# A two-layer hybrid trunk with experts: weights laid out row by row for their transfers, and the split of the experts' weights left to VectorE

## The chip, the cores and the metric

The kernel runs on one core of one Trainium2 chip. The core has a matrix engine (TensorE, PE in the rows; its weight loads are PEld), three engines for elementwise work (VectorE = DVE, ScalarE = ACT, GpSimd = POOL), a queue engine (SyncE = SP) that issues most transfers, and 16 DMA engines that move data between device memory (DRAM) and the core's memory (SBUF). The metric is device microseconds of one execution. Before the change the median of 3 runs is 2021.1 us (2020.6 to 2021.52).

## The reference

Two layers work on 256 tokens of 1024 channels. Each layer has a mixing part (dilated attention and a gated delta rule, both fed by one input projection, merged by gates, then an output projection and a layer norm) and a channel part. The channel part of layer 0 is a dense SwiGLU. That of layer 1 sends each token to 2 of 8 experts:

```python
def swiglu(x, w_gate, w_up, w_down):
    return (jax.nn.silu(x @ w_gate) * (x @ w_up)) @ w_down
...
    for e in range(N_EXPERTS):
        y = y + gates[..., e:e + 1] * swiglu(x, w_gate[e], w_up[e], w_down[e])
```

An expert has three matrices of 1024 x 3584 (the last one transposed), in float32. All 8 experts are computed, so 352 MB of their weights pass through the core once, beside some 144 MB of weights of the two mixing parts and of the dense channel part.

## The kernel before, in words

**Weights.** All weights go through one object, `Stream` (`W`). They are cut into pieces of two blocks of 128 rows and 512 columns: 128 partitions x 2 x 512 float32, 512 KB. `plan` lists the pieces in the order of their use. For each piece:

- `dma_to` issues the transfer on SP, into a 4 KB-per-partition slot named `raw` (L82). In DRAM the weights lie as the reference has them, so a partition of a piece is two runs of 2 KB. In the experts' part every third piece (`n_dma % HALVES == 0`) goes instead into two 2 KB slots named `rawh`, by two transfers of 256 KB (L79).
- `advance` splits the float32 values exactly into a high part `whi` (a float32r copy by ScalarE, L102 for a whole piece, L100 twice for a `rawh` piece) and a low part `wlo` (raw minus high, L105). For a whole piece VectorE does L105 once over 128x1024. For a `rawh` piece VectorE does the first half and GpSimd the second, 128x512 each. The same sharing, on whole slots, is used for every piece while `share` is set, which is the case from the output projection of layer 1 to the end of the first gate product of the experts' part.
- `gemm` (L414 to L416) makes three products for each block of 128 rows: high x by high w, high x by low w, low x by high w. So one piece is 2 x 3 products of 512 columns for each tile of tokens. In the experts' part an expert has one tile of at most 128 tokens; the mixing parts have two tiles.

`caps(raw, spl)` bounds how many pieces are loaded ahead (raw) and how many are split ahead (spl). In the experts' part they are (18, 5), then (21, 5). The slots come from two pools: `k4` with 36 slots of 4 KB (raw, whi, wlo, the gathered tokens `xe`, the hidden values `hte`, the split copies of x) and `k2` with 16 slots of 2 KB (rawh, `mgs`, the one-hot rows `Pt`, and others).

**The experts' part.** An expert's 3584 hidden columns are taken in 7 chunks of 512. A chunk is 12 pieces: 4 of gate (result `mg`), 4 of up (`mu`), and 4 of down (`oe`) for the chunk before. When `mu` is complete, VectorE multiplies it into `mgs` (L1322), TensorE turns `mgs` in four transposes (`ht`, L1335), and ScalarE and VectorE split that into `hte` (L1338, L1339), which the down products of the chunk read. At an expert's end `scatter` scales its two result halves (L1348 on ScalarE, L1349 on VectorE, `oh` and `ol`), two products per tile spread them over the tokens (`sc`, L1353 and L1354), and VectorE adds them to x (L1356). For every second expert the tokens of the next pair are gathered (`xe`, L1286).

**Order.** The program is written as one main line of products and a set of generators that are stepped between them; a scheduler then fixes each engine's order when the kernel is built. Every engine works through its own list in order and waits on semaphores. A change of what one engine does can therefore move instructions on the others.

The functions that the change touches, with what calls them:

Of the kernel before, what the change touches and what calls it, by code (L numbers as in the profile page):

```python
# [18 lines left out]
P = 128  # L19
# [24 lines left out]

class Stream:
    """Weights in the order of their use, in pieces of two row blocks: DRAM to SBUF, then their float32 values
    split exactly into two float32r parts. caps() bounds the pieces loaded ahead and those split ahead."""

    def __init__(self, k, raw, spl):
        self.k, self.raw_cap, self.spl_cap = k, raw, spl  # L50
        self.subs = []
        self.key = {}
        self.raw = {}
        self.split = {}
        self.n_dma = 0
        self.n_split = 0
        self.retired = 0
        self.done_subs = set()
        self.share = False
        self.moe = 0  # L60
        self.SHARE, self.HALVES = 3, 3

    def caps(self, raw, spl):
        self.raw_cap, self.spl_cap = raw, spl

    def add(self, key, src, kb, n):
        first = len(self.subs)
        for h in range(0, kb, 2):
            self.subs.append((src[:, h:h + 2], n))
        self.key[key] = list(range(first, len(self.subs)))  # L70

    def dma_to(self, i):
        while self.n_dma <= min(i, len(self.subs) - 1):
            src, n = self.subs[self.n_dma]
            q = self.k.nc.sync
            if self.n_dma >= self.moe and self.n_dma % self.HALVES == 0:
                t = [self.k.k2([P, 512], name="rawh") for _ in range(2)]
                for k in range(2):
                    q.dma_start(t[k][:, :n], src[:, k])  # L79
            else:  # L80
                t = self.k.k4([P, 2, 512], name="raw")
                q.dma_start(t[:, :, :n], src)  # L82
# [43 lines left out]
class Kern:  # L126
# [7 lines left out]
    # ---------------------------------------------------------------- interleaving  # L134
# [46 lines left out]
    # ---------------------------------------------------------------- small helpers  # L181
# [36 lines left out]
    # ---------------------------------------------------------------- constants  # L218
# [47 lines left out]
        # rows of an odd block of 16 and columns of the block before it  # L266
# [18 lines left out]
    def rope_tables(self):  # L285
        """cos and sin of position * frequency, with the angle reduced exactly by multiples of 2 pi."""
# [25 lines left out]
        # [c | c] and [-s | s]  # L312
# [33 lines left out]
    # ---------------------------------------------------------------- weight plan  # L346
    def plan(self):
        W, A = self.W, self.A

        def sq(w, r0, kb, c0, n):  # L350
            return w[r0 * P:(r0 + kb) * P, c0:c0 + n].rearrange("(k p) n -> p k n", p=P)

        for l in range(DEPTH):
            wi = A["w_in"][l]
            for kg in range(2):
                W.add(("at", l, 0, 0, kg), sq(wi, 4 * kg, 4, 0, 512), 4, 512)
            for half in range(2):
                for part in range(3):
                    for kg in range(2):
                        W.add(("qb", l, half, part, kg), sq(wi, 4 * kg, 4, C_QB + part * 1024 + half * 512, 512), 4, 512)  # L360
            for g in range(3):
                for part in range(1 if g == 0 else 0, 3):
                    for kg in range(2):
                        W.add(("at", l, g, part, kg), sq(wi, 4 * kg, 4, part * 1536 + g * 512, 512), 4, 512)
                for nm, c0 in ((("z", C_Z),), (), (("ga", C_GA), ("gb", C_GB)))[g]:
                    for f in range(2):
                        for kg in range(2):
                            W.add((nm, l, f, kg), sq(wi, 4 * kg, 4, c0 + f * 512, 512), 4, 512)
            for f in range(2):
                W.add(("ba", l, f, 0), sq(A["w_branch_a"][l], 0, 4, f * 512, 512), 4, 512)  # L370
                for kg in range(2):
                    W.add(("bb", l, f, kg), sq(A["w_branch_b"][l], 4 * kg, 4, f * 512, 512), 4, 512)
            for kg in range(2):
                for f in range(2):
# [1213 lines left out]
```

## Time and profile before

| | |
|---|---|
| median of 3 runs | 2021.1 us |
| profiled execution, first to last instruction | 2023.3 us |
| PE busy | 1960.1 us (97%) |
| PEld busy | 1640.3 us (81%) |
| DVE busy | 1644.2 us (81%) |
| ACT busy | 1270.8 us (63%) |
| POOL busy | 613.9 us (30%) |
| HBM read | 506.09 MB, 253 GB/s over the span |

The profile page is of one execution, whose span of 2023.3 us stands beside the 2021.1 us of the runs. The experts' part is the second half of the span: the rows of 40 slices show that DMA goes from about half busy to 9 tenths near slice 20, and that DVE goes up with it. A product's busy time in these rows (0.39 us) is longer than the distance from its start to the next one's start (0.23 us), because products are pipelined; distances between starts are read from the timeline.

### The profile page before, as it was taken

The page shows a single profiled execution, that of the slowest core. Times are in us where ns is not written, and L with a number is a line of the kernel's source. Part 1 is how long each engine was busy: PE and PEld are TensorE (multiplying, and loading weights), DVE is VectorE, ACT ScalarE, POOL GpSimd, SP SyncE. Part 2 cuts the span into 40 slices and gives each one's busy share as a digit, 9 for nine tenths or more (in the row PEclk, how much of TensorE's full clock was granted, in tenths as well). Part 3 has the DMA queues.
Part 4 walks back from the last instruction along what each step waited for, and adds up shares of the span by engine and source line. Part 5 has one row for each costly group of instructions (what it writes and reads, how often), then busy time and mean ns, then how long its engine had stood idle before and what let it go on. Part 6 is the DMA issues. An engine that isn't in the chain of part 4 may idle for free. (4 is left out here: it accounts for less than half of the span.)

```text
span 2023.3 us, 30086 instructions
## 1 busy us (share of the span) xinstructions
PE 1960.1 (97%) x10143; PEld 1640.3 (81%) x10143; DVE 1644.2 (81%) x2208; ACT 1270.8 (63%) x1958; POOL 613.9 (30%) x484
## 2 busy tenths in 40 slices
PE   8889999999999999999999999999999999999995
PEld 7878888888888878888788788887888878888784
DVE  7886757665566976666789989999899998999997
ACT  5554546444444555554388778777787777877784
POOL 4341211000003422210334334343343433434342
PEclk9899999999999999999999999999999999999998
DMA  8344344664664353537589999999999999999991
GB/s 297 105 157 150 132 132 154 197 222 131 236 215 127 118 177 95 181 127 239 205 292 373 354 350 347 363 366 350 350 357 359 366 355 334 371 358 370 351 351 42
DMA packets 278544, 513.65 MB, mean 254 GB/s; under 512 B 29904, under 2 KB 32176, under 8 KB 278384
## 3 DMA queue, kind: packets, MB, share of 16 engines
q1 hardware_dynamic: 276144, 504.11, 70.6%
q0 software_dynamic: 2240, 7.56, 1.1%
q8 instruction: 81, 1.33, 0.3%
q14 instruction: 79, 0.65, 0.1%
HBM read 506.09 MB, written 5.51 MB: 253 GB/s over the span
## 5 line engine op out<-in xcount | busy, mean ns | idle before, releaser
L105 DVE TENSOR_TENSOR wlo<-raw,whi 128x1024 fp32r<-128x1024 f32 (+1 forms) x726 | 921.7, 1291 | 121.4 <-ACT whi L102 118.5
L102 ACT CAST whi<-raw 128x1024 fp32r<-128x1024 f32 (+1 forms) x726 | 744.8, 1046 | 78.0 <-DVE wlo L105 18.9
L105 POOL TENSOR_TENSOR wlo<-rawh,whi 128x512 fp32r<-128x512 f32 x224 | 390.7, 1744 | 593.4 <-ACT whi L100 415.3
L105 DVE TENSOR_TENSOR wlo<-rawh,whi 128x512 fp32r<-128x512 f32 x224 | 269.1, 1201 | 6.3 <-ACT whi L100 6.3
L100 ACT CAST whi<-rawh 128x512 fp32r<-128x512 f32 x448 | 256.1, 622 | 18.8 <-PE mg L415 9.8
L415 PE MATMUL oe<-wlo,hte 128*128 128x512 f32 x448 | 180.7, 403 | 0.4
L415 PE MATMUL mu<-wlo,xe 128*128 128x512 f32 x440 | 172.6, 392 | 6.6 <-DVE wlo L105 6.3
L414 PE MATMUL oe<-whi,hte 128*128 128x512 f32 x448 | 175.7, 392 | 0.0
L416 PE MATMUL oe<-whi,hte 128*128 128x512 f32 x448 | 175.2, 391 | 0.0
L414 PE MATMUL mu<-whi,xe 128*128 128x512 f32 x440 | 171.6, 390 | 0.0
L416 PE MATMUL mu<-whi,xe 128*128 128x512 f32 x440 | 171.5, 390 | 0.0
L414 PE MATMUL mg<-whi,xe 128*128 128x512 f32 x440 | 171.4, 390 | 0.0
L416 PE MATMUL mg<-whi,xe 128*128 128x512 f32 x440 | 171.4, 390 | 0.0
L415 PE MATMUL mg<-wlo,xe 128*128 128x512 f32 x440 | 171.3, 389 | 0.0
L105 POOL TENSOR_TENSOR wlo<-raw,whi 128x512 fp32r<-128x512 f32 x53 | 84.3, 1603 | 102.5 <-ACT whi L102 84.0
L566 PE MATMUL qb<-xhl,whi 128*128 128x256 f32 x384 | 113.4, 296 | 0.0
L569 PE MATMUL qb<-xhl,whi 128*128 128x256 f32 x384 | 110.9, 289 | 0.0
L571 PE MATMUL qb<-xhl,wlo 128*128 128x256 f32 x384 | 110.8, 289 | 0.0
L414 PE MATMUL at<-whi,xhl 128*128 128x512 f32 x256 | 108.1, 422 | 0.0
L415 PE MATMUL at<-wlo,xhl 128*128 128x512 f32 x256 | 102.6, 401 | 3.3 <-DVE wlo L105 3.3
L415 PEld LDWEIGHTS mu<-wlo,xe 128*128 128x128 f32 x440 | 82.6, 188 | 28.4 <-DVE wlo L105 10.9
L416 PE MATMUL at<-whi,xhl 128*128 128x512 f32 x256 | 101.9, 398 | 0.0
(421 smaller groups left out, 3875.7 us busy)
## 6 DMA issues: line engine op xcount, KB each, us to landing
raw<-in_w_in SPq DMA_DIRECT2D x168, 512.0 KB
raw<-in_moe_w_gate SPq DMA_DIRECT2D x168, 512.0 KB
raw<-in_moe_w_up SPq DMA_DIRECT2D x167, 512.0 KB
raw<-in_moe_w_down SPq DMA_DIRECT2D x113, 512.0 KB
rawh<-in_moe_w_down SPq DMA_DIRECT2D x222, 256.0 KB
rawh<-in_moe_w_up SPq DMA_DIRECT2D x114, 256.0 KB
rawh<-in_moe_w_gate SPq DMA_DIRECT2D x112, 256.0 KB
raw<-in_ffn_w_down SPq DMA_DIRECT2D x22, 512.0 KB
```

The costliest lines, as they stand in the source:

```text
L100: k.last_act = nc.scalar.copy(hi[:, a:b, :n], r[:, :, :n])
L102: k.last_act = nc.scalar.copy(hi[:, :, :n], raw[:, :, :n])
L105: ins = (nc.gpsimd if share and a else nc.vector).tensor_tensor(lo[:, a:b, :n], r[:, :, :n], f32(hi)[:, a:b, :n], op=OP.subtract)
L414: nc.tensor.matmul(o, lhsT=xh, rhs=hi[:, kk, :n], start=st, stop=False)
L415: nc.tensor.matmul(o, lhsT=xh, rhs=lo[:, kk, :n], start=False, stop=False)
L416: nc.tensor.matmul(o, lhsT=xl, rhs=hi[:, kk, :n], start=False, stop=en)
L566: nc.tensor.matmul(o, lhsT=hi[:, kk, w], rhs=self.xhl[k // 2][:, k % 2, :S], start=(k == 0 and b % 2 == 0), stop=False, skip_group_check=True)
L569: nc.tensor.matmul(o, lhsT=hi[:, kk, w], rhs=self.xhl[k // 2][:, k % 2, S:], start=False, stop=False, skip_group_check=True)
L571: nc.tensor.matmul(o, lhsT=lo[:, kk, w], rhs=self.xhl[k // 2][:, k % 2, :S], start=False, stop=(k == 7), skip_group_check=True)
```

## The change

The host lays the weights out anew before the launch, and the kernel gets two arrays in place of ten weight inputs. In `trunk` and `moe` each piece is one block of 128 x 1024 float32 that holds, for each partition, the 4 KB that belong into its slot, in the order of use within a layer or an expert. The 16 columns of `w_in` that `load_layer_small` reads become an input of their own, `w_ba`. A transfer of a piece is then 128 rows of 4 KB from 512 KB that lie together, rather than 256 runs of 2 KB.

`SHARE`, `HALVES` and the `rawh` slots are gone: in the experts' part every piece is loaded by one transfer into a `k4` slot, copied by one ScalarE instruction and split by one VectorE instruction. GpSimd still takes half of a low part while `share` is set. The caps of the experts' part go from (18, 5) and (21, 5) to (12, 5). `overflow` (experts with more than 128 tokens; it does not run on this input) reads the new arrays. Comments are left out of the new file, so its line numbers differ: L105 becomes L150, L102 becomes L148, L1322 becomes L1332 and so on.

```diff
+def moe_pieces(nm, c, j):
+
+    first = 12 * c + {"mg": 0, "mu": 4, "md": 8}[nm] + 2 * j
+    return first, first + 1
+
+
+def lay_out(inputs):
+
+    def piece(w, r0, c0, n):
+        return w[..., r0 * P:(r0 + 2) * P, c0:c0 + n].reshape(w.shape[:-2] + (2, P, n)).swapaxes(-3, -2).reshape(
+            w.shape[:-2] + (P, 2 * n))
+    blocks = [(w, l, r0 + h, c0, n) for _, w, l, r0, kb, c0, n in trunk_blocks() for h in range(0, kb, 2)]
+    trunk = np.zeros((len(blocks), P, 1024), np.float32)
+    for i, (w, l, r0, c0, n) in enumerate(blocks):
+        trunk[i, :, :2 * n] = piece(inputs[w][l], r0, c0, n)
...
-            q = self.k.nc.sync
-            if self.n_dma >= self.moe and self.n_dma % self.HALVES == 0:
-                t = [self.k.k2([P, 512], name="rawh") for _ in range(2)]
-                for k in range(2):
-                    q.dma_start(t[k][:, :n], src[:, k])
-            else:
-                t = self.k.k4([P, 2, 512], name="raw")
-                q.dma_start(t[:, :, :n], src)
+            t = self.k.k4([P, 2, 512], name="raw")
+            self.k.nc.sync.dma_start(t[:, :, :n], src[:, :2 * n].rearrange("p (k n) -> p k n", k=2))
...
-            share = self.share or (i >= self.moe and i % self.SHARE == 0)
-            if isinstance(raw, list):
-                parts = [(raw[j][:, None], j, j + 1) for j in range(2)]
-                for r, a, b in parts:
-                    k.last_act = nc.scalar.copy(hi[:, a:b, :n], r[:, :, :n])
-            else:
-                k.last_act = nc.scalar.copy(hi[:, :, :n], raw[:, :, :n])
-                parts = [(raw[:, j:j + 1], j, j + 1) for j in range(2)] if share else [(raw, 0, 2)]
-            for r, a, b in parts:
+            share = self.share
+            k.last_act = nc.scalar.copy(hi[:, :, :n], raw[:, :, :n])
+            for r, a, b in [(raw[:, j:j + 1], j, j + 1) for j in range(2)] if share else [(raw, 0, 2)]:
...
-        self.CAP_MOE0 = (18, 5)
-        self.CAP_MOE = (21, 5)
+        self.CAP_MOE0 = (12, 5)
+        self.CAP_MOE = (12, 5)
```

The scheduler's order is the same on PE and DVE up to the output projection of layer 1. From there it changes at many places. Three of them follow.

On VectorE at the end of the first expert, before the change (`wlo` is the low part of a piece, from `raw` a whole piece and from `rawh` the first half of one; `x` with `sc` are the four adds of the scatter):

```order
L1339 TENSOR_TENSOR hte<-ht,hte 128x4x128
L105 TENSOR_TENSOR wlo<-rawh,whi 128x512
L105 TENSOR_TENSOR wlo<-raw,whi 128x1024
L1349 SCALAR_TENSOR_TENSOR ol<-oe,gs,oh 128x512
L105 TENSOR_TENSOR wlo<-raw,whi 128x1024
L1356 TENSOR_TENSOR x_9358<-x_9358,sc 128x512
L1356 TENSOR_TENSOR x_9359<-x_9359,sc 128x512
L1349 SCALAR_TENSOR_TENSOR ol<-oe,gs,oh 128x512
L105 TENSOR_TENSOR wlo<-rawh,whi 128x512
L1356 TENSOR_TENSOR x_9358<-x_9358,sc 128x512
L1356 TENSOR_TENSOR x_9359<-x_9359,sc 128x512
L105 TENSOR_TENSOR wlo<-raw,whi 128x1024 x2
```

And on VectorE at the same place with the change:

```order
L1359 SCALAR_TENSOR_TENSOR ol<-oe,gs,oh 128x512
L150 TENSOR_TENSOR wlo<-raw,whi 128x1024
L1366 TENSOR_TENSOR x_9358<-x_9358,sc 128x512
L150 TENSOR_TENSOR wlo<-raw,whi 128x1024
L1349 TENSOR_TENSOR hte<-ht,hte 128x4x128
L150 TENSOR_TENSOR wlo<-raw,whi 128x1024 x2
L1366 TENSOR_TENSOR x_9359<-x_9359,sc 128x512
L150 TENSOR_TENSOR wlo<-raw,whi 128x1024
L1359 SCALAR_TENSOR_TENSOR ol<-oe,gs,oh 128x512
L150 TENSOR_TENSOR wlo<-raw,whi 128x1024
L1366 TENSOR_TENSOR x_9358<-x_9358,sc 128x512
L1366 TENSOR_TENSOR x_9359<-x_9359,sc 128x512
```

The six instructions of the scatter stood within two whole pieces and one half piece; now they stand among six whole pieces, and an `hte` comes between them.

On TensorE within a chunk of the first expert, from the last product of `mu` to the transposes of the hidden values, before the change:

```order
L416 MATMUL mu<-whi,xe 128x512
L415 MATMUL oe<-wlo,hte 128x512
L416 MATMUL oe<-whi,hte 128x512
L414 MATMUL oe<-whi,hte 128x512
L415 MATMUL oe<-wlo,hte 128x512
L416 MATMUL oe<-whi,hte 128x512
L414 MATMUL oe<-whi,hte 128x512
L415 MATMUL oe<-wlo,hte 128x512
L416 MATMUL oe<-whi,hte 128x512
L414 MATMUL oe<-whi,hte 128x512
L1335 MATMUL ht<-ident,mgs 128x128 x4
```

And on TensorE at the same place with the change:

```order
L426 MATMUL mu<-whi,xe 128x512
L424 MATMUL oe<-whi,hte 128x512
L425 MATMUL oe<-wlo,hte 128x512
L426 MATMUL oe<-whi,hte 128x512
L424 MATMUL oe<-whi,hte 128x512
L425 MATMUL oe<-wlo,hte 128x512
L426 MATMUL oe<-whi,hte 128x512
L424 MATMUL oe<-whi,hte 128x512
L1345 MATMUL ht<-ident,mgs 128x128 x4
```

Nine products of `oe` stood between the last `mu` and the transposes; now there are seven.

On VectorE at the layer norm behind the output projection of layer 1, token tile 1, before the change (`xhl` are the split, transposed parts of the normalized tile 0):

```order
L213 TENSOR_TENSOR xhl<-tp,xhl 128x2x128 x4
L1127 SCALAR_TENSOR_TENSOR x_9359<-x_9359,wo 128x512
L1049 BN_STATS bnst<-x_9359 128x6
L105 TENSOR_TENSOR wlo<-raw,whi 128x512
L1127 SCALAR_TENSOR_TENSOR x_9359<-x_9359,wo 128x512
L1049 BN_STATS bnst<-x_9359 128x6
```

And with the change:

```order
L1137 SCALAR_TENSOR_TENSOR x_9359<-x_9359,wo 128x512
L258 TENSOR_TENSOR xhl<-tp,xhl 128x2x128
L1059 BN_STATS bnst<-x_9359 128x6
L258 TENSOR_TENSOR xhl<-tp,xhl 128x2x128
L1137 SCALAR_TENSOR_TENSOR x_9359<-x_9359,wo 128x512
L258 TENSOR_TENSOR xhl<-tp,xhl 128x2x128 x2
L150 TENSOR_TENSOR wlo<-raw,whi 128x512
L1059 BN_STATS bnst<-x_9359 128x6
```

The four `xhl` stood ahead of the sums of tile 1; now they are spread among them. On TensorE the transposes that feed them come 17 products of `wo` later than before.

## Rows read from the trace of the kernel before

**Rows 1.** The page's busy times and its 40 slices (each digit tenths of a slice of 50.6 us; GB/s by slice).

```profile
PE 1960.1 (97%) x10143; PEld 1640.3 (81%) x10143; DVE 1644.2 (81%) x2208; ACT 1270.8 (63%) x1958; POOL 613.9 (30%) x484
...
PEclk9899999999999999999999999999999999999998
DMA  8344344664664353537589999999999999999991
```

**Rows 2.** Busy times by stretch of 100 us: first the length, then PE, PEld, DVE, ACT, POOL in us with the number of instructions, the granted TensorE clock, the share of the DMA engines, GB/s.

```profile
400.00:500.00 100.00, 100.00 (x462) 82.84 (x461) 61.99 (x81) 45.12 (x63) 2.00 (x2) 1.00 0.59 189
...
1300.00:1400.00 100.00, 99.90 (x454) 82.23 (x454) 95.10 (x86) 77.21 (x106) 39.76 (x23) 1.00 1.01 375
...
1500.00:1600.00 100.00, 99.62 (x446) 81.48 (x445) 96.89 (x89) 78.78 (x109) 40.95 (x23) 1.00 1.00 363
```

**Rows 3.** TensorE's timeline in the experts' part at three places (start, length, what, and in brackets idle time of the engine and what ended it): around a wait at 1155 us, within a chunk at 1407 to 1410 us, and at the transposes of the two chunks behind that.

```profile
1154.80 0.39 PE L416 MATMUL mu<-whi,xe 128*128 128x512 f32 x1
1155.03 0.40 PE L414 MATMUL mu<-whi,xe 128*128 128x512 f32 x1
1156.83 0.50 PE L415 MATMUL mu<-wlo,xe 128*128 128x512 f32 x1 [1.41 <-DVE wlo L105]
1157.17 0.39 PE L416 MATMUL mu<-whi,xe 128*128 128x512 f32 x1
...
1407.46 0.39 PE L416 MATMUL mu<-whi,xe 128*128 128x512 f32 x1
...
1409.50 0.39 PE L414 MATMUL oe<-whi,hte 128*128 128x512 f32 x1
1409.74 0.60 PE L1335 MATMUL ht<-ident,mgs 128*128 128x128 f32 x4
...
1426.60 0.60 PE L1335 MATMUL ht<-ident,mgs 128*128 128x128 f32 x4
...
1443.43 0.60 PE L1335 MATMUL ht<-ident,mgs 128*128 128x128 f32 x4
```

**Rows 4.** Who waited for whom between 1060 and 1975 us, all rows of PE, and the first rows of ACT: us in total, times, longest.

```profile
PE mu L415 <- DVE wlo L105: 6.3, 7, 1.4
...
ACT mgs L1317 <- DVE wlo L105: 64.2, 21, 4.8
ACT mgs L1317 <- POOL wlo L105: 34.4, 31, 1.6
ACT PT L1306 <- PE PT L1303: 15.8, 7, 3.1
ACT whi L102 <- PE mg L415: 15.6, 25, 0.6
```

**Rows 5.** VectorE's and GpSimd's timeline at the first of these waits.

```profile
1152.70 0.68 DVE L105 TENSOR_TENSOR wlo<-rawh,whi 128x512 fp32r<-128x512 f32 x1
1153.83 1.29 DVE L1356 TENSOR_TENSOR x<-x,sc 128x512 f32<-128x512 f32 x2 [0.45 <-PE sc L1354]
1155.03 2.88 DVE L105 TENSOR_TENSOR wlo<-raw,whi 128x1024 fp32r<-128x1024 f32 x2
...
1154.41 1.29 POOL L105 TENSOR_TENSOR wlo<-rawh,whi 128x512 fp32r<-128x512 f32 x1 [1.65 <-ACT whi L100]
```

**Rows 6.** Groups of instructions between 1060 and 2000 us, shapes apart: count, busy us, mean ns of one, idle time before them.

```profile
L105 DVE TENSOR_TENSOR wlo<-raw,whi 128x1024 fp32r<-128x1024 f32 x425 | 571.5, 1369 | 14.6 <-ACT whi L102 14.4
...
L105 POOL TENSOR_TENSOR wlo<-rawh,whi 128x512 fp32r<-128x512 f32 x213 | 373.7, 1754 | 566.7 <-ACT whi L100 390.9 <-DVE wlo L105 48.7 <-DMA raw<-in_moe_w_gate 34.9
L105 DVE TENSOR_TENSOR wlo<-rawh,whi 128x512 fp32r<-128x512 f32 x213 | 258.4, 1213 | 5.9 <-ACT whi L100 5.9
...
L415 PE MATMUL oe<-wlo,hte 128*128 128x512 f32 x431 | 174.1, 404 | 0.4
...
L1322 DVE TENSOR_TENSOR mgs<-mgs,mu 128x512 f32<-128x512 f32 x53 | 36.3, 685 | 16.6 <-ACT whi L100 11.9 <-PE mu L416 2.4 <-issue 2.3
L1339 DVE TENSOR_TENSOR hte<-ht,hte 128x512 fp32r<-128x512 f32 x53 | 36.0, 678 | 0.0
```

**Rows 7.** Line L105 on VectorE, between 1100 and 1950 us: durations in ns, least, median, most; and the timeline of VectorE at 1408 to 1412 us.

```profile
L105 DVE TENSOR_TENSOR wlo<-raw,whi x385: 1206/1212/2321, 1099.0 to 1949.0; 128x1024 fp32r<-128x1024 f32 x193
...
1407.96 0.69 DVE L1322 TENSOR_TENSOR mgs<-mgs,mu 128x512 f32<-128x512 f32 x1 [0.31 <-PE mu L416]
...
1411.41 2.35 DVE L105 TENSOR_TENSOR wlo<-raw,whi 128x1024 fp32r<-128x1024 f32 x2
```

**Rows 8.** What the DMA engines moved between 1300 and 1310 us and, below it, between 20 and 30 us; then two 512 KB transfers with the median us from issue to landing; then what the SP queue waited for most between 1060 and 2000 us.

```profile
DMA packets 1986, 3.76 MB, mean 376 GB/s; under 512 B 152, under 2 KB 152, under 8 KB 1986
...
DMA packets 2107, 4.06 MB, mean 406 GB/s; under 512 B 126, under 2 KB 126, under 8 KB 2107
...
lnb<-in_ln_b POOLq DMA_DIRECT2D x3, 512.0 KB, 7.8
...
SPq L79 <- DVE wlo L105: 238.2, 136, 5.7
```

**Rows 9.** What PE waited for in the first 40 us, and ScalarE's copies of the first pieces.

```profile
PE at L435 <- ACT xhl L212: 1.9, 1, 1.9
...
15.37 1.05 ACT L102 CAST whi<-raw 128x1024 fp32r<-128x1024 f32 x1 [1.63 <-DMA raw<-in_w_in]
...
18.02 1.04 ACT L102 CAST whi<-raw 128x1024 fp32r<-128x1024 f32 x1 [1.61 <-DMA raw<-in_w_in]
```

**Rows 10.** The end of the last expert, PE, ACT and DVE.

```profile
1992.02 0.66 PE L1335 MATMUL ht<-ident,mgs 128*128 128x128 f32 x4 [1.63 <-DVE mgs L1322]
1992.71 0.59 ACT L1338 CAST hte<-ht 128x512 fp32r<-128x512 f32 x1 [3.30 <-PE ht L1335]
1994.16 0.68 DVE L1339 TENSOR_TENSOR hte<-ht,hte 128x512 fp32r<-128x512 f32 x1
```

**Rows 11.** TensorE at the layer norm behind the output projection of layer 1: the first transposes of token tile 0.

```profile
987.27 0.63 PE L207 MATMUL tp<-ident,x 128*128 128x128 f32 x4 [0.51 <-issue]
```

More of the change, by code (lines that the diff above doesn't have):

```diff
@@ L42, in hlf, with trunk_blocks, sq @@
     return f
+def trunk_blocks():
+    for l in range(DEPTH):
+        def sq(key, c0, n=512):
+            for kg in range(2):
+                yield key + (kg,), "w_in", l, 4 * kg, 4, c0, n
+        yield from sq(("at", l, 0, 0), 0)
+        for half in range(2):
+            for part in range(3):
+                yield from sq(("qb", l, half, part), C_QB + part * 1024 + half * 512)
+        for g in range(3):
+            for part in range(1 if g == 0 else 0, 3):
+                yield from sq(("at", l, g, part), part * 1536 + g * 512)
+            for nm, c0 in ((("z", C_Z),), (), (("ga", C_GA), ("gb", C_GB)))[g]:
+                for f in range(2):
+                    yield from sq((nm, l, f), c0 + f * 512)
+        for f in range(2):
+            yield ("ba", l, f, 0), "w_branch_a", l, 0, 4, f * 512, 512
+            for kg in range(2):
+                yield ("bb", l, f, kg), "w_branch_b", l, 4 * kg, 4, f * 512, 512
+        for kg in range(2):
+            for f in range(2):
+                yield ("wo", l, f, kg), "w_out", l, 4 * kg, 4, f * 512, 512
+        if l % 2 == 0:
+            for c in range(6):
+                n = min(512, D_FF - c * 512)
+                for nm, w in (("fg", "ffn_w_gate"), ("fu", "ffn_w_up")):
+                    for kg in range(2):
+                        yield (nm, c, kg), w, 0, 4 * kg, 4, c * 512, n
+            for kg in range(6):
+                for f in range(2):
+                    yield ("fd", kg, f), "ffn_w_down", 0, 4 * kg, min(4, 22 - kg * 4), f * 512, 512
@@ new lines, in moe_pieces @@
+def moe_pieces(nm, c, j):
[9 more added lines that the diff above has]
+        trunk[i, :, :2 * n] = piece(inputs[w][l], r0, c0, n)
+    moe = np.empty((NE, 84, P, 1024), np.float32)
+    for c in range(7):
+        for j in range(2):
+            for h in range(2):
+                for nm, w in (("mg", "moe_w_gate"), ("mu", "moe_w_up")):
+                    moe[:, moe_pieces(nm, c, j)[h]] = piece(inputs[w][0], 4 * j + 2 * h, 512 * c, 512)
+                moe[:, moe_pieces("md", c, j)[h]] = piece(inputs["moe_w_down"][0], 4 * c + 2 * h, 512 * j, 512)
+    return {"trunk": trunk, "moe": moe}
@@ new lines, in plan @@
+        first = 0
+        for key, _, _, _, kb, _, n in trunk_blocks():
+            W.add(key, [A["trunk"][first + j] for j in range(kb // 2)], n)
+            first += kb // 2
+        prev = None
+        for e in range(NE):
+            for c in range(7):
+                for nm in ("mg", "mu"):
+                    for kg in range(2):
+                        W.add((nm, e, c, kg), [A["moe"][e, j] for j in moe_pieces(nm, c, kg)], 512)
+                if prev:
+                    for f in range(2):
+                        W.add(("md",) + prev + (f,), [A["moe"][prev[0], j] for j in moe_pieces("md", prev[1], f)], 512)
+                prev = (e, c)
@@ L402, in gemm @@
+        for f in range(2):
+            W.add(("md",) + prev + (f,), [A["moe"][prev[0], j] for j in moe_pieces("md", prev[1], f)], 512)
     def gemm(self, keys, accs, x, first=True, last=True, tiles=(0, 1)):
@@ L1480, in overflow @@
                     a = {}
-                    for nm in ("moe_w_gate", "moe_w_up"):
+                    for nm in ("mg", "mu"):
                         a[nm] = self.acc(nm)
                         for kg in range(2):
-                            wt = load(nm, kg * 512, c * 512)
+                            wt = load(nm, c, kg)
                             for kk in range(4):
@@ L1496, in overflow @@
                     for f in range(2):
-                        wt = load("moe_w_down", c * 512, f * 512)
+                        wt = load("md", c, f)
                         for kk in range(4):
@@ L1577 @@
     arrays, aps = {}, {}
-    for name in _INS:
+    inputs = {name: np.asarray(a) for name, a in inputs.items()}
+    inputs["w_ba"] = inputs["w_in"][:, :, C_BA:C_BA + 16]
+    inputs.update(lay_out(inputs))
+    for name in _INS + ["w_ba", "trunk", "moe"]:
         a = np.ascontiguousarray(inputs[name])
```

72 lines of the change are left out of this document (9 added, 63 removed).

## The prediction

> **What bounds the kernel now.** I read the busy times and slices first. PE is busy 97% of the span at full granted clock, but a product's busy time is longer than its slot, so this does not yet say that it is the bound; DMA is at 9 tenths in the whole experts' part [rows 1]. The stretches of 100 us show four candidates there at once: PE 99.6 to 99.9, VectorE 95 to 97, the DMA engines 1.00 to 1.01, ScalarE 77 [rows 2]. What decides is the timeline of TensorE and its waits. Undisturbed products start 0.23 us apart (1154.80, 1155.03), and a chunk without gather or scatter, from one set of transposes to the next, takes 16.83 us (1426.60 to 1443.43) [rows 3]. That is 72 products of 0.227 us (16.3) and the four transposes with the slower product behind them: nothing in it is a wait. Over 915 us of the experts' part PE waited 7 times and 6.3 us in all, each time for a low part from VectorE; the first rows of ScalarE's waits name no transfer [rows 4]. So TensorE bounds the experts' part, VectorE touches it at a few places, and the transfers do not touch it at all: SP itself waits most for a slot that VectorE still has to free [rows 8].
>
> The wait at 1155.03 shows how the touch comes about. VectorE does the scatter's adds, waiting in between for their products, while GpSimd holds a half piece from 1154.41 to 1155.70; the two whole pieces behind that take 2.88 us instead of 2.35 [rows 5, 7], and the product that needs the first of them comes 1.41 us late [rows 3].
>
> **The low halves on VectorE.** Between 1060 and 2000 us VectorE did 425 whole pieces at 1.369 us and 213 half pieces at 1.213 us; GpSimd did the other 213 halves at 1.754 us [rows 6]. Now VectorE does 638 whole pieces. Their price has two ends: 1.369 us, the mean, and 1.21 us, least and median in the same part [rows 7]. I take 1.21: a distribution with median 1.212 and most 2.321 is a fixed length with collisions on top, and GpSimd is the only engine whose work goes away.
>
> The Trainium skill, SBUF — State Buffer, section Who interferes with whom, says that a VectorE instruction with two inputs in SBUF and a GpSimd instruction that reads SBUF block each other for the whole instruction. By that rule a half piece on VectorE costs a half piece plus up to one of GpSimd's, and all of it ends with the change; without the rule one would keep 1.369.
>
> Per clean chunk VectorE then has 12 x 1.21 + 0.685 + 0.678 (the `mgs` and `hte` rows [rows 6]) = 15.9 us against 8 x 1.369 + 4 x 1.213 + 1.36 = 17.2 before, in the 16.83 us that TensorE needs. (Durations of neighbours overlap by some 0.07 us, so 17.2 fits into 16.83 with nothing to spare.) So VectorE gets about 1.3 us of room per chunk. With 1.369 it would have 17.8, 0.6 us more than now: 55 chunks (8 experts of 7, less the first) x 0.6 = 33 us slower, the upper end of this term.
>
> What the room is worth: each of PE's waits costs its idle time and a restart. From 1155.03 to 1157.17 there are 2.14 us for two slots of 0.23, a loss of 1.68 for 1.41 idle [rows 3], so 0.27 more. 6.3 + 7 x 0.27 + 0.4 of idle before `oe` products [rows 6] = 8.6 us. This is all that the experts' part can give, whatever else is freed. The scatter's own 4 adds and 2 splits stay, though spread among six whole pieces instead of standing together; I take **7.5 us**, bounds 0 and 8.6.
>
> **ScalarE.** A chunk goes from 8 whole copies and 8 half copies to 12 whole ones. It was busy 77 to 79 of 100 us [rows 2]; the change lowers that. Nothing, hidden behind TensorE; if its cover goes it is still the least loaded of the three.
>
> **Rows of 4 KB, one transfer per piece.** In a clean chunk 12 pieces of 0.524 MB in 16.83 us are 374 GB/s, which the trace shows as 375 and 376 [rows 2, 8]. With the same 2 KB rows it shows 406 GB/s between 20 and 30 us [rows 8], so the demand is met now and longer rows bring the experts' part nothing. If 4 KB rows were 10% worse, 365 GB/s would still hold the 363 of a stretch with gather and scatter [rows 2], with the pieces loaded ahead as cover; beyond that it would cost. I take 0, and 0 for the caps: 12 pieces ahead are 12 x 1.4 = 16.8 us, and the slowest 512 KB load that shows its landing took 7.8 us [rows 8].
>
> At the start it is different. ScalarE waits 1.6 us each for the pieces at 15.37 and 18.02, and PE stands 1.9 us behind the second of them, for an `xhl` copy that ScalarE has queued after it [rows 9]. A piece now is half as many runs to issue and to move. I take **1 us**, bounds 0 and 1.9. The rest of the two mixing parts keeps its order and its splits, and there PE waits for VectorE and ScalarE; 0.
>
> **The end.** PE stood 1.63 us for the last `mgs` behind a `wlo` of VectorE [rows 10], 1.9 with the restart. In the new order 13 more products of `oe` come ahead of these transposes, 3.0 us, which covers it; but only two products that don't need the last `hte` are left behind them. In the rows ScalarE's half of `hte` is done 1.28 us and VectorE's 2.82 us after the transposes begin [rows 10], the latter with two whole pieces ahead of it, of which one is left. 0.87 us of cover (transposes and two products) leaves a wait of about 0.8. I take a gain of **1 us**, bounds 1.9 and a loss of 0.3.
>
> **The layer norm before the experts.** VectorE does the `xhl` splits of tile 0 (128x256, half the size of the half piece of 0.68 us [rows 5]) among the sums of tile 1, so tile 1 can be later by about 1 us; TensorE's transposes of tile 0 come 17 products later, which takes away the 0.51 us that PE stood for them [rows 11]. 0, bounds 1 either way.
>
> Sum: 7.5 + 1 + 1 = 9.5 us off the span of 2023.3, so 2013.8 us. The runs' median stands 2.2 us below that execution: **2011.6 us**. With all bounds on the good side (8.6 + 1.9 + 1.9 + 1) it is 13.4, 2007.7; with the bad ones, without VectorE's upper end, 2020 to 2022.
>
> **Rivals.** *The waits stay.* They all come near a scatter, whose adds wait for products; if these, not GpSimd, make the low parts late, VectorE's room does not help where it is needed and only the 1 to 2 us at the ends remain: 2019 to 2021. For it: 0.45 us idle before the adds [rows 5]. Against: the 0.53 us that the two pieces lose directly behind GpSimd's half, and that the adds now alternate with pieces.
>
> *Slower: the transposes come too early.* Seven instead of nine `oe` products stand between the end of `mu` and the transposes. In the rows the last `mu` begins at 1407.46 and the transposes at 1409.74, while `mgs` runs from 1407.96 to 1408.65 [rows 3, 7]: 1.1 us to spare, which becomes 0.6. VectorE works in order, and a whole piece of 1.21 us that starts just before `mu` is done puts `mgs` back by up to that. From 0.6 us of delay on PE stands in every chunk: 0.3 us of idle and 0.27 of restart in 55 chunks are 31 us, less the 9.5: 2043. In half of the chunks: 2027. Against it: VectorE has 0.9 us to spare in a chunk and is mostly waiting for `mu` when its turn comes (idle 16.6 us before the 53 `mgs`, all for others [rows 6]).
>
> *Much faster: TensorE is not the bound.* PEld is busy only 82% in the experts' part [rows 2]. If that were 18% of headroom, VectorE (95 to 97 busy) would be the bound, and its 1.3 us of 17.2 would come off: 7.6% of some 970 us is 73 us, 1948 us. Against: between 400 and 500 us, where no other engine is over 62 busy, PEld is at 82.84 with PE at 100 [rows 2]; 83% is its ceiling here. The Trainium skill, Perfetto Trace Analysis, section Identifying the Most-Contended Engine, says to judge headroom by the LDWEIGHTS share instead of the matmul share; by that rule this rival would hold, and the trace disagrees with it as far as 100% is taken for the ceiling.
>
> **How the numbers follow.** Forecast 0.70; waits stay 0.16; transposes too early, or VectorE at its upper price, 0.11; much faster 0.03. The forecast's own range is 2007 to 2017. The range reaches over the second case and its bounds: 2005 to 2021, which leaves out the slower case, the much faster one and a little at the edges. What counts as no change here is 0.2%, 2017.1 to 2025.1 us. Faster: 0.03 and nearly all of the forecast's 0.70, 0.71. Same: most of the second case and the forecast's bad edge, 0.17. Slower: 0.12.
>
> **What would show it.** In the changed profile: L150 on VectorE at about 1.21 us with its most near it; VectorE's busy share in the experts' part near 89 instead of 95; PE's waits for `wlo` there under 2 us; `ht` with no waits but at the end; the same 16.8 us for a clean chunk. Wrong it would be by rows of `ht <- DVE mgs` with tens of waits, by ScalarE waiting for `raw`, by L150 near 1.37, or by a clean chunk that is not 16.8 us.

## The result, and the profile after

The changed kernel takes 2044.0 us, median of 4 runs (2042.2 to 2044.5), against 2021.1: a ratio of 1.0112 with an interval of 1.0098 to 1.0127. It is slower by some 23 us; 2011.6 with a range of 2005 to 2021 was predicted, so time and sign are wrong.

The profiled span went from 2023.3 to 2042.1 us, 18.8 more. A span is some 1.8 us shorter than its run's time (2042.1 for 2043.9), so the profiled execution of before would be a run of about 2025.1, some 4 us above the median: those 4 of the 23 us do not show between the two spans. Where the rest arises is read from the sets of transposes `ht` of the experts' part, the second and the last: here before the change (with one product behind a set), then after it.

```profile
1039.45 0.60 PE L1335 MATMUL ht<-ident,mgs 128*128 128x128 f32 x4
...
1426.95 0.49 PE L415 MATMUL oe<-wlo,hte 128*128 128x512 f32 x1
```

```profile
1039.92 0.60 PE L1345 MATMUL ht<-ident,mgs 128*128 128x128 f32 x4
...
1563.88 0.60 PE L1345 MATMUL ht<-ident,mgs 128*128 128x128 f32 x4
...
1576.51 0.39 PE L424 MATMUL mu<-whi,xe 128*128 128x512 f32 x1
1576.84 0.50 PE L425 MATMUL mu<-wlo,xe 128*128 128x512 f32 x1
1577.17 0.40 PE L426 MATMUL mu<-whi,xe 128*128 128x512 f32 x1
...
1581.08 0.60 PE L1345 MATMUL ht<-ident,mgs 128*128 128x128 f32 x4
1581.57 0.50 PE L425 MATMUL oe<-wlo,hte 128*128 128x512 f32 x1
...
2014.73 0.60 PE L1345 MATMUL ht<-ident,mgs 128*128 128x128 f32 x4
```

Up to the second set the two profiles differ by 0.5 us, but the start of an execution differs by more than that from one to the next (the output projection of layer 1 begins at 962.6 to 967.5 us in the 14 profiles). From the first product of that projection on, it is 73.2 us to the second set (966.74 to 1039.92) instead of 72.0 (967.45 to 1039.45), 1.2 more.

```profile
967.45 0.39 PE L435 MATMUL wo<-whi,mT 128*128 128x512 f32 x1
```

```profile
966.74 0.39 PE L445 MATMUL wo<-whi,mT 128*128 128x512 f32 x1
```

From the second set to the last it is 974.8 us instead of 952.6 ([rows 10] have the last set of before, at 1992.02), 22.2 more. But 13 `oe` products that stood behind the last transposes now stand ahead of them, 13 x 0.227 = 3.0 us that are only moved, so this part lost 19.3 us. Behind the last set it is 27.4 instead of 31.3, 3.9 less, with these 3.0 in it. A clean chunk takes 17.20 us (1563.88 to 1581.08) instead of the 16.83 of [rows 3]. The extra 0.38 us lies at two places: a `mu` product whose low part comes late (0.33 and 0.33 us to the next starts instead of 0.23, and a few slots of 0.235 behind them, some 0.24 in all), and the product behind the transposes, which starts 0.49 us after them (1581.57) where before it was 0.35 (1426.95, behind the 1426.60 of [rows 3]): 0.14. None of it is a big wait, and TensorE's list of waits shows almost nothing. The busy times, first of the whole span, then by stretch as in [rows 2]:

```profile
PE 1981.7 (97%) x10143; PEld 1636.7 (80%) x10143; DVE 1581.9 (77%) x2208; ACT 1246.3 (61%) x1734; POOL 225.3 (11%) x263
...
1300.00:1400.00 100.00, 99.71 (x443) 79.90 (x443) 85.74 (x81) 70.59 (x79) 0.00 (x0) 1.00 0.99 364
1500.00:1600.00 100.00, 99.07 (x437) 78.64 (x436) 86.61 (x85) 73.71 (x84) 0.00 (x0) 1.00 0.98 357
```

In these stretches every engine became less busy, at full clock: 443 products in 100 us where there were 454. PEld shows the lost slots better (82.2 to 79.9) than PE (99.9 to 99.7), whose products stretch over a gap. Who waited for whom between 1060 and 1990 us:

```profile
ACT mgs L1327 <- PE mg L426: 140.7, 52, 3.7
DVE wlo L150 <- ACT whi L148: 82.4, 75, 3.2
...
DVE mgs L1332 <- PE mu L426: 29.8, 48, 0.7
...
PEld mu L425 <- DVE wlo L150: 24.3, 56, 1.0
...
PE mu L425 <- DVE wlo L150: 4.3, 7, 0.6
PE mg L425 <- DVE wlo L150: 2.1, 7, 0.3
```

In [rows 4] ScalarE waited before `mgs` for a slot that a low part had to free. It stood there as often as now (21 + 31 waits, 98.6 us in all), but with eight of the next pieces copied, and the clean chunk had no loss by it. Now it waits for TensorE's sum `mg`, once per chunk, with four copied. Its timeline and VectorE's in the same chunk:

```profile
1573.99 0.60 ACT L1327 ACTIVATE mgs<-mg 128x512 f32<-128x512 f32 x1 [3.66 <-PE mg L426]
1574.48 7.68 ACT L148 CAST whi<-raw 128x1024 fp32r<-128x1024 f32 x8
1582.07 0.57 ACT L1348 CAST hte<-ht 128x512 fp32r<-128x512 f32 x1
```

```profile
1575.56 3.50 DVE L150 TENSOR_TENSOR wlo<-raw,whi 128x1024 fp32r<-128x1024 f32 x3 [1.57 <-ACT whi L148]
1579.69 0.69 DVE L1332 TENSOR_TENSOR mgs<-mgs,mu 128x512 f32<-128x512 f32 x1 [0.63 <-PE mu L426]
1580.29 5.76 DVE L150 TENSOR_TENSOR wlo<-raw,whi 128x1024 fp32r<-128x1024 f32 x5
```

ScalarE stands 3.66 us at the SiLU (L1327), for the product that ends the gate sum, with eight copies `whi` queued behind it; then it does these eight in a row. VectorE has nothing to split meanwhile (1.57 us), and TensorE uses up what was split ahead until the product at 1576.84 comes late. In the built order the SiLU stands four `whi` pieces behind the chunk's `hte`; before the change, eight. On VectorE the multiply (L1332) stands seven low parts behind `hte` instead of eight (those of GpSimd counted): it waits for `mu`, and the low part for 1581.57 is queued behind it.

### The profile page after: what moved, and what is told of

It reads as the page before. It is cut to its first block, busy times and chain, and to the rows that moved or that the text cites. A ratio compares the mean times of both kernels' runs of the same rounds, so it can differ in the third digit from the quotient of the medians.

```text
span 2042.1 us, 28745 instructions
## 1 busy us (share of the span) xinstructions
PE 1981.7 (97%) x10143; PEld 1636.7 (80%) x10143; DVE 1581.9 (77%) x2208; ACT 1246.3 (61%) x1734; POOL 225.3 (11%) x263
## 5 line engine op out<-in xcount | busy, mean ns | idle before, releaser
L150 DVE TENSOR_TENSOR wlo<-raw,whi 128x1024 fp32r<-128x1024 f32 (+1 forms) x950 | 1098.4, 1201 | 194.5 <-ACT whi L148 191.3
L148 ACT CAST whi<-raw 128x1024 fp32r<-128x1024 f32 (+1 forms) x950 | 942.7, 1045 | 84.0 <-PE oe L425 31.0
L425 PE MATMUL mu<-wlo,xe 128*128 128x512 f32 x440 | 178.7, 406 | 4.3 <-DVE wlo L150 4.3
L1063 POOL TENSOR_TENSOR bnmv<-bnmv,mhalf 128x1 f32<-128x1 f32 x8 | 7.0, 871 | 1112.2 <-DVE bnmv L1062 1112.2
L1327 ACT ACTIVATE mgs<-mg 128x512 f32<-128x512 f32 x55 | 32.9, 598 | 148.7 <-PE mg L426 148.7
L425 PEld LDWEIGHTS oe<-wlo,hte 128*128 128x128 f32 x448 | 84.0, 188 | 23.2 <-DVE wlo L150 1.0
L425 PEld LDWEIGHTS mg<-wlo,xe 128*128 128x128 f32 x440 | 82.6, 188 | 24.5 <-DVE wlo L150 8.0
```

The lines of the kernel that those rows point to most:

```text
L150: ins = (nc.gpsimd if share and a else nc.vector).tensor_tensor(lo[:, a:b, :n], r[:, :, :n], f32(hi)[:, a:b, :n], op=OP.subtract)
L425: nc.tensor.matmul(o, lhsT=xh, rhs=lo[:, kk, :n], start=False, stop=False)
L1063: nc.gpsimd.tensor_tensor(mv[:, 3:4], mv[:, 2:3], self.mhalf[:, 0:1], op=OP.pow)
L1327: nc.scalar.activation(g, res["mg"], AF.Silu)
```

## The experiments

"Pieces" are `whi` on ScalarE, or `wlo` on VectorE, between a chunk's `hte` and its SiLU or multiply. All ratios are to the kernel before on the same chip (2019.5 to 2020 us).

**Holding the SiLU back** (e1_pin):

```diff
+        with self.behind(self.W.k.last_act):
-        nc.scalar.activation(g, res["mg"], AF.Silu)
+            nc.scalar.activation(g, res["mg"], AF.Silu)
```

> The changed kernel, with one thing more: ScalarE's SiLU of a chunk (mgs) is held behind the copy of the piece that was split last when it is written, so 8 pieces instead of 4 stand between hte and mgs on ScalarE, as before the change. Everything else of the change stays (GpSimd out, 12 pieces ahead, 4 KB rows). Theory O (the SiLU moved too far ahead on ScalarE, which stands 3.7 us per chunk for mg with the copies of the next pieces behind it): a clean chunk goes back from 17.20 to about 16.83 us, and the time to 2012 to 2021 us. Theory V (VectorE lacks GpSimd's help): stays at 2044. Theory C (12 pieces ahead, or the new rows, make pieces late): stays at 2044.

2022.7 us, 1.0013 (1.0004 to 1.0023), a little above the expected range; the clean chunk is as expected. The SiLU stands behind eight pieces, the clean chunk is 16.82 us, and the stretch between the two sets of transposes 953.0, with the 13 products behind it again, as before the change. That returns some 20 of the 23 us (1.0112 to 1.0013) without GpSimd and with the new rows and caps. But the order shows that the multiply moved along, to eight, and the transposes from seven `oe` products behind `mu` to ten, so the run alone does not say which of the three it was.

**Parts of the change by themselves**: the slots `rawh` taken out of the kernel before, with caps of (12, 5) (e2_norawh); GpSimd's part alone taken out (e3_noshare); the new rows in DRAM alone (e4_layout).

```diff
e2: self.SHARE, self.HALVES = 3, 100000   CAP_MOE0 = CAP_MOE = (12, 5)
e3: self.SHARE, self.HALVES = 100000, 3
e4: lay_out() and its plan, all else as before
```

> The kernel before, with the rawh slots alone removed: each piece of the experts' part is loaded by one transfer into a k4 slot, and the caps are (12, 5), which the k4 slots need; GpSimd still takes half of every third low part, and the weights lie as they did. In its built order 4 pieces stand between hte and mgs on ScalarE, as with the change. Theory O: slow, 2035 to 2048 us, with a clean chunk near 17.2 us. Theory V: as before, 2021 us, since GpSimd still helps. Theory C by the rows of 4 KB: 2021; by the caps: 2044, which e1 tells apart.

> The kernel before, with GpSimd's part alone taken away: rawh slots, caps (21, 5) and layout stay, VectorE does both halves of the rawh pieces. Between hte and mgs on ScalarE stand 8 pieces as before. Theory O: not slower than before, 2010 to 2021 us, with VectorE at about 1.21 us for a whole piece. Theory V: 2035 to 2044 us. Theory C: 2021.

> The kernel before on the new layout alone: rows of 4 KB for whole pieces, rawh pieces by two transfers of 2 KB rows, GpSimd's part and the caps (18, 5) and (21, 5) as before. Built order in the experts' part as before. Theory O and V: 2020 to 2022 us, the start perhaps 1 us earlier. Theory C by the rows: slower, up to 2044.

e4 is 1.0000 (0.9990 to 1.0009): the rows are worth nothing here (the `rawh` third keeps its 2 KB rows in it). e3 is 2017.5 us, 0.9987 (0.9977 to 0.9997), e2 is 2106.8, 1.0427 (1.0407 to 1.0447). In e2's order the SiLU stands behind four pieces, in e3's and e4's behind eight. The caps alone (an order that was built and not run) leave it behind eight in 40 of 55 chunks and put it behind five in 13. So it is mainly the loss of the `rawh` slots that moves it. Why can be argued, not shown: `mgs` lives in the 2 KB pool that `rawh` filled, in [rows 4] the SiLU waits for a slot there, and without `rawh` one is always free. e2 is far slower than the change itself, which has the same four pieces but no GpSimd, and than any side expected.

**The same hold on e2** (f2_share_pin).

> The kernel of e2_norawh (the one before without rawh slots, GpSimd still taking half of every third low part), with the SiLU held behind eight pieces. Theory O: the 87 us of e2_norawh came from the early SiLU, GpSimd's 1.75 us for a half piece only made the late pieces later; held back, the clean chunk is 16.8 to 17.0 as in the kernel before, 2019 to 2026 us. Rival G (GpSimd's sharing of 4 KB slots itself costs it): clean chunk near 18.6, 2090 us or more.

2045.1 us, 1.0126 (1.0109 to 1.0143). Most clean chunks return to 16.8 to 17.2 us from 18.66, but 25 us stay, mostly in the chunks with scatter and gather. Neither side's number: 62 of e2's 87 us go with the hold, and GpSimd has a price of its own (g3, below).

**Which of the moved instructions.** The SiLU held behind five pieces (f1_five) and seven (g2_seven) with the multiply left at seven, and only the multiply held (g1_silu4).

```diff
+            self.acts.append(k.last_act)
...
f1:      with self.behind(self.W.acts[-4]):
g2:      with self.behind(self.W.acts[-2]):
             nc.scalar.activation(g, res["mg"], AF.Silu)
...
g1:      with self.behind(self.W.dves[-4]):
             nc.vector.tensor_tensor(g, g, res["mu"], op=OP.mult)
```

> The changed kernel, with the SiLU held on ScalarE behind five pieces (whi) after hte instead of four; nothing else differs, and seven products of oe still stand between mu and the transposes. Theory O (ScalarE reaches the SiLU before TensorE has finished the gate sums, so the copies behind it come late, and TensorE runs out of split pieces by 0.38 us in every chunk): one piece more ahead lasts TensorE 6 x 0.227 = 1.36 us, more than the 0.38 that is missing, so the whole loss goes at once: clean chunk 16.82, about 2022.7 us like e1_pin, ratio 1.000 to 1.003. Rival P (the loss is proportional to how far the SiLU stands ahead): three quarters of the 21.3 us stay, 2038 us. Rival T (the transposes of the hidden values stand too early on TensorE, seven oe products behind mu, the slower rival of the prediction): e1_pin also moved these from seven to ten, and here they stay at seven, so 2044 us.

> The changed kernel with the SiLU left where it is on ScalarE (behind four pieces), and only VectorE's multiply of mgs held behind eight low parts instead of seven; the transposes then stand behind ten oe products, as in e1_pin. In the changed kernel a clean chunk loses 0.38 us at two places: about 0.24 at the mu products whose low part comes late behind the SiLU, and 0.14 behind the transposes, where the low part stands behind a multiply that waits for mu (f1_five still has that 0.14). Theory O+M (both instructions stand too early, each costs its own part): clean chunk 17.06, about 2033 us. Rival M (the multiply alone): 16.82, 2023 us. Rival O (the SiLU alone): 17.20, 2044 us.

> The changed kernel with the SiLU held behind seven pieces on ScalarE; VectorE's multiply stays behind seven low parts, where the changed kernel has it (e1_pin: eight and eight). Theory O+M: the SiLU costs nothing more than at five, the multiply still its 0.14 in each clean chunk: 16.95, 2028 to 2032 us. Rival O by steps (17.20 at four pieces, 16.95 at five, then nothing): 16.82, 2023 us.

| kernel | SiLU behind | multiply behind | clean chunk | second to last `ht` | less moved products | ratio |
|---|---|---|---|---|---|---|
| changed | 4 | 7 | 17.20 us | 974.8 us | 971.9 us | 1.0112 |
| g1_silu4 | 4 | 8 | 17.09 | 968.3 | 965.4 | 1.0079 |
| f1_five | 5 | 7 | 16.96 | 963.5 | 960.8 | 1.0061 |
| g2_seven | 7 | 7 | 17.01 | 965.7 | 963.0 | 1.0067 |
| e1_pin | 8 | 8 | 16.82 | 953.0 | 953.0 | 1.0013 |

In the changed kernel and g1 13 more `oe` products stand ahead of the last transposes than in e1 and in the kernel before, in f1 and g2 12; the sixth column takes them off at 0.227 us each.

f1 refutes the expectation that the SiLU is the whole cause, and the proportional one too: at five pieces its own part is gone, and what is left does not fall further at seven, though f1's ScalarE still stands 84.2 us at the SiLU and g2's only 8.5 (first line f1, second g2):

```profile
ACT mgs L1330 <- PE mg L428: 84.2, 48, 2.7
```

```profile
ACT mgs L1330 <- PE mg L428: 8.5, 28, 0.3
```

That rest is VectorE's multiply, as f1's VectorE and TensorE show:

```profile
1070.88 0.69 DVE L1335 TENSOR_TENSOR mgs<-mgs,mu 128x512 f32<-128x512 f32 x1 [1.51 <-PE mu L428]
1071.48 3.49 DVE L152 TENSOR_TENSOR wlo<-raw,whi 128x1024 fp32r<-128x1024 f32 x3
...
1072.27 0.60 PE L1348 MATMUL ht<-ident,mgs 128*128 128x128 f32 x4
1072.76 0.50 PE L427 MATMUL oe<-wlo,hte 128*128 128x512 f32 x1
```

The low part that was held up behind the multiply ends 1.22 us after 1071.48, and its product starts at 1072.76, 0.13 us late. With the multiply right and the SiLU at four (g1) a clean chunk keeps 0.27 us of its 0.38. So both instructions stood too early. In the sixth column the multiply alone costs 7.8 to 10.0 us (f1, g2 less e1), the SiLU alone 12.4 (g1 less e1), both together 18.9; by the ratios of the runs it is 9.7 to 10.9, 13.3 and 20.0, each within some 4 us. g1 and g2 came out slower than either was expected to (2037.2 for 2033, 2035.0 for at most 2032), though each is nearest to the theory of both. The transposes moved with the multiply in every run (seven `oe` products behind `mu`, or ten), so no run parts the two. By the traces it is the multiply: in none of the five did TensorE wait for `mgs` at these transposes.

**Why e1 and e3 gain so little.** e3 came out in its expected range, at 2.4 us less than before. In e1 ScalarE waits in the same way at another place, and in e3 the waits at the scatter remain; first e1's timelines, then who TensorE waited for in e3:

```profile
1126.52 0.37 ACT L1316 CAST PT<-PT 128x256 fp32r<-128x256 f32 x1 [7.73 <-PE PT L1313]
1126.79 0.59 ACT L1349 CAST hte<-ht 128x512 fp32r<-128x512 f32 x1
1127.27 3.90 ACT L148 CAST whi<-raw 128x1024 fp32r<-128x1024 f32 x4
...
1129.65 0.50 PE L425 MATMUL mg<-wlo,xe 128*128 128x512 f32 x1 [0.74 <-DVE wlo L150]
```

```profile
PE mu L415 <- DVE wlo L105: 4.8, 8, 0.8
PE oe L415 <- DVE wlo L105: 1.1, 3, 0.4
```

f3_pt holds the copy `PT` behind three pieces; f4_pt_adds also issues the scatter's adds one step later. g4_before_held has both holds and nothing of the change.

```diff
+        with self.behind(self.last_act):
-        nc.scalar.copy(PT, ps[:, :S])
+            nc.scalar.copy(PT, ps[:, :S])
...
+            yield
+            with self.behind(self.last_dve):
-            nc.vector.tensor_tensor(ys, ys, ps, op=OP.add)
+                nc.vector.tensor_tensor(ys, ys, ps, op=OP.add)
```

> e1_pin with one more instruction held on ScalarE: the copy PT (the turned one-hot rows of an expert), which e1_pin has directly ahead of hte and for whose transposes ScalarE idles 46.5 us in 7 places, up to 7.7 each. Behind three pieces now. Theory O at a second place: TensorE's seven gaps of 1.13 us at the wlo behind it (1128.51 and so on) go, 7 x 0.91 = 6.3 us: 2016.4 us, ratio 0.997 to 0.999. Rival S (the waits are made by the scatter's adds on VectorE, and come back at the next place): 2021 to 2023 us.

> f3_pt with the four adds of each scatter on VectorE issued one step later, so that their products are done when VectorE comes to them. If the adds' waits for sc (0.45 to 1.35 us each in the profiles so far) make the low parts behind them late, TensorE's other seven gaps of 0.64 us (1147.85 and so on) go as well, 7 x 0.41 = 2.9 us: about 2013.5 us. If these gaps come from oh on ScalarE instead, the same as f3_pt within 0.1%.

> The kernel before, with PT on ScalarE and the scatter's adds on VectorE held as in f4_pt_adds, nothing of the change in it. If the adds' place alone made the seven waits of 6.3 us (8.6 with their restarts), they go without the change: 2012 to 2014 us, and f4's gain is not the change's. If GpSimd's halves are needed for them, they stay: 2018 to 2021 us.

f3: 2016.3 us, 0.9981 (0.9971 to 0.9990). f4: 2014.1 us, 0.9973 (0.9961 to 0.9984); TensorE then has no listed wait at all between 1060 and 1980 us, and the stretch between the sets of transposes is 943.5 us, 9.1 less than in the kernel before. g4: 2021.7 us, 1.0010 (1.0000 to 1.0019), 954.0 us, the same seven waits. So these holds bring nothing without the change, and the change, mended, is the faster kernel, though by little, some 5.5 us by the runs (3.2 to 7.9 by the interval). Two limits stand. The intervals of f3 and f4 overlap, so what the adds bring rests on the traces (945.8 and 943.5 us between the sets); and in f3 they do not wait for `sc`, as the expectation supposed, but only stand ahead of a piece that TensorE needs. And in g4 the hold did not take the adds off their products: VectorE still waits for them there, more than before (8.4 us in 14 waits), so g4 does not show what well placed adds would bring without the change.

```profile
DVE x L1359 <- PE sc L1355: 12.0, 14, 2.1
```

**GpSimd's part alone** (g3_share, f4 with GpSimd sharing every third piece again):

```diff
-            share = self.share
+            share = self.share or (i >= 278 and i % 3 == 0)
```

> f4_pt_adds with GpSimd computing half of every third low part again, as in the kernel before, but from whole slots. It prices the removed part of the change under an order without early instructions. Theory G (GpSimd's half takes 1.75 us and slows VectorE's pieces, and what is short of pieces becomes late): f2_share_pin stands 22 us over e1_pin with the same kind of order, the PT wait is gone from both, so some 12 to 20 us over f4: 2026 to 2034 us. Rival (GpSimd's part costs only where something else is late already): 2014 to 2017 us.

2036.6 us, 1.0084 (1.0066 to 1.0101), 22.6 over f4 and a little more than expected. The low parts between 1060 and 2000 us in g3, below them in f4, and last in e3, the kernel before without GpSimd's part:

```profile
L150 DVE TENSOR_TENSOR wlo<-raw,whi 128x1024 fp32r<-128x1024 f32 x421 | 586.5, 1419 | 15.6 <-PE xe L1296 11.2 <-ACT whi L148 4.4
L150 POOL TENSOR_TENSOR wlo<-raw,whi 128x512 fp32r<-128x512 f32 x211 | 341.9, 1620 | 598.5 <-ACT whi L148 224.7 <-PE oe L425 160.7 <-PE mu L426 83.3
L150 DVE TENSOR_TENSOR wlo<-raw,whi 128x512 fp32r<-128x512 f32 x210 | 226.1, 1077 | 7.0 <-ACT whi L148 7.0
```

```profile
L150 DVE TENSOR_TENSOR wlo<-raw,whi 128x1024 fp32r<-128x1024 f32 x638 | 740.1, 1218 | 20.6 <-ACT whi L148 18.0
```

```profile
L105 DVE TENSOR_TENSOR wlo<-raw,whi 128x1024 fp32r<-128x1024 f32 x424 | 506.6, 1221 | 15.5 <-ACT whi L102 14.7
L105 DVE TENSOR_TENSOR wlo<-rawh,whi 128x512 fp32r<-128x512 f32 x424 | 273.6, 687 | 9.6 <-ACT whi L100 9.1 <-DMA rawh<-in_moe_w_gate 0.5
```

With GpSimd's help VectorE spends 586.5 + 226.1 = 812.6 us on the low parts, without it 740.1 us for all of them. In the kernel before it was 571.5 + 258.4 = 829.9 us [rows 6], and 506.6 + 273.6 = 780.2 in e3, but there taking GpSimd away brought only 2.4 us. So the 22.6 us are the price in f4's order; g3's clean chunks mostly stay at 16.82 us, and the loss lies in the chunks with scatter and gather.

## Why the prediction was wrong, point by point

**TensorE as the bound** held: with the order mended its slots are 0.227 us, it is 100% busy between 1300 and 1400 us in f4, and a clean chunk is 16.82 us. "Much faster" falls.

```profile
1300.00:1400.00 100.00, 100.00 (x456) 82.38 (x454) 88.33 (x86) 74.52 (x84) 0.00 (x0) 1.00 0.98 369
```

**"ScalarE. ... Nothing, hidden behind TensorE"** is the step that failed. It counted ScalarE's busy time, 77 to 79 of 100 us, and took the rest for cover; it did not look at its order, of which no place was read. The rows of before had the numbers. Their clean chunk has eight pieces ahead of the SiLU, and these two lines:

```profile
1435.48 0.39 PE L416 MATMUL mg<-whi,xe 128*128 128x512 f32 x1
...
1440.30 0.60 ACT L1317 ACTIVATE mgs<-mg 128x512 f32<-128x512 f32 x1 [2.52 <-DVE wlo L105]
```

ScalarE came to the SiLU at 1440.30 - 2.52 = 1437.8, when `mg` had been complete for 1.9 us (1435.48 + 0.39). Four pieces fewer, at TensorE's pace of 6 x 0.227 = 1.36 us each, are 5.4 us earlier: a wait of 3.5 us in each chunk (3.66 measured), out of ScalarE's 22% of 16.8 us, 3.7, of idle time. So one wait uses up the cover, and it comes while only four of the next pieces are copied; the 2.52 us of before came behind eight. By itself this measured 12.4 us (13.3 by the runs), and the multiply, for which no term stood in the sum at all, 7.8 to 10.0 (9.7 to 10.9).

**The low halves on VectorE.** The price of 1.21 us was right: 1.220 us mean in the changed kernel, least and most of L150 1215 and 1227 ns. g3 shows the collision behind it: with GpSimd's halves the mean of the whole pieces goes from 1.22 to 1.42 us, and nothing else was changed from f4. The Trainium skill, SBUF — State Buffer, section Who interferes with whom, which the prediction weighed against the mean, says that a VectorE instruction with two inputs in SBUF contends with a GpSimd instruction that reads SBUF. These rows agree with that; how long one blocks the other they do not show. The gain of 7.5 us does not follow from this step alone: in e3, GpSimd's part removed and eight pieces kept ahead of the SiLU, TensorE has 5.9 us of waits instead of 6.3, and the runs gain 2.4 us. (Its 951.9 us between the sets of transposes hold 11 products, 2.5 us, that were moved ahead of the last set; without them it is 949.4 for 952.6.) That is the rival "the waits stay", and its cause is there in e3: the adds still wait for their products.

```profile
DVE x L1356 <- PE sc L1354: 10.5, 11, 1.4
```

In the order of the change this cause is gone: in the changed kernel, e1 and f3 no add is listed as waiting for `sc`. TensorE's waits came back at other places, in e1 seven behind `PT` (0.74 us) and seven of 0.24 us behind an add that stood ahead of a needed piece without waiting. With `PT` and the adds held the stretch gains 9.1 us, a little over the upper bound of 8.6. (e4, with the order of before, has 952.0 in place of 952.6, so some 0.6 of it can be chance.)

**Rows of 4 KB and caps: 0.** Right for the rows (e4). Fewer pieces ahead did no harm to the loads: ScalarE waited 0.6 us for transfers in the whole experts' part, e1 and f4 run with 12. What the caps alone cost by the order was not run.

**The two ends and the layer norm.** The gain of 1 us at the start did not come. The 1.9 us wait is gone in the changed kernel and a later one for `bar` is 4.2 instead of 2.9 us, but that is so in e3 too, which has the old rows, while e4, with the new ones, has 1.5 and 4.2: the wait of 1.9 belonged to one execution and not to the rows. At the end the mechanism was right: the wait of 1.63 us for the last `mgs` is gone (the set at 2014.73 above has none), and behind it the products come later than back to back. The last `oe` begins 7.83 us after the transposes instead of 10.09, 2.26 less where 13 products fewer are 2.95, a loss of 0.7 for the 0.8 foretold. The layer norm cost 1.2 us, for a term of 0 with a bound of 1: the 0.51 us that tile 0 stood is gone, as said, but the transposes of tile 1 follow 1.91 us of idle time, where before they had 0.49.

```profile
998.63 0.63 PE L207 MATMUL tp<-ident,x 128*128 128x128 f32 x4 [0.49 <-issue]
...
2002.11 0.40 PE L416 MATMUL oe<-whi,hte 128*128 128x512 f32 x1
```

```profile
PE ba L504 <- ACT bar L499: 4.2, 1, 4.2
...
999.03 1.23 PE L252 MATMUL tp<-ident,x 128*128 128x128 f32 x7 [1.91 <-issue]
...
2022.56 0.39 PE L426 MATMUL oe<-whi,hte 128*128 128x512 f32 x1
```

**The slower rival** gave 2043 us and the result is 2044, but not by its mechanism. It feared that VectorE would come late to `mgs` and TensorE stand at `ht`; `ht` has no wait. VectorE came early to `mgs` and stood there itself, and the pieces behind were late. That the two numbers meet is luck. **The list of signs** was half right: L150 at 1.21 and no waits at `ht` came true, "waits for `wlo` under 2 us" (6.4) and "16.8 for a clean chunk" did not. VectorE's share is 86 to 87, 88.3 in f4, for the 89 foretold. No sign was set on ScalarE waiting for TensorE.

## What to carry to other kernels

An engine that works in order can hold up the bound with a fifth of its time free: before an engine is put down as covered, look in the new order for each of its instructions that reads another engine's result, and work out from the trace when it is reached and when its input is ready. Removing a buffer can move such instructions (here, as argued above, because the full pool was what held them back). When waits at one place are to be removed, ask for each engine in the chain what its next instruction would wait for; here GpSimd, the SiLU, the multiply, `PT` and the adds each had to be right before the 9 us appeared in the experts' part (some 5.5 in the runs).

## What the runs showed of the hardware that was not expected

Help can cost: GpSimd taking a sixth of the low parts lengthened VectorE's total for them by 72 us (812.6 against 740.1) and the kernel by 22.6; in the order of before it was 50 us (829.9 against 780.2) and 2.4, so a longer total alone does not give the price. A low part that makes its product start 0.1 us late costs about 0.24 us on TensorE: the late product's own slot is 0.33 too instead of 0.23 (1576.84 to 1577.17), and the next few run at about 0.235 before 0.227 is reached again. And half the DMA packets, each of twice the bytes, brought nearly the same bytes in the experts' part; in [rows 8] ten microseconds took 1986 packets and 3.76 MB, here:

```profile
DMA packets 1005, 3.67 MB, mean 367 GB/s; under 512 B 112, under 2 KB 112, under 8 KB 1004
```
